# A hybrid decoder layer on one Trainium2 core: the weights of the overflow branch are loaded through the GpSimd queue instead of the SP queue

## The chip, the cores and the metric

The kernel runs on one core of one Trainium2 chip. The metric is the device time of one execution in microseconds (us). Three runs of the kernel before took 947.99, 948.39 and 949.15 us, so its median is 948.39 us. The execution that was profiled took 947.23 us, of which 945.5 us lie between its first and last instruction.

## What is computed

One decoder layer for 256 tokens of width 2048 in float32: an input projection, attention beside a convolution, an output projection, a normalisation, a mixture of experts, a second normalisation and a gated embedding. The change lies in the mixture of experts. The reference, cut to it:

```python
g_logits = t @ wg + bg                              # top-1 of 4 groups
g_top = jnp.argmax(g_logits, axis=-1)
e_in = (t @ we + be).reshape(T, 4, 8)[..., g_top]   # the 8 experts of that group
top_p, top_i = lax.top_k(softmax(e_in), 2)          # 2 experts a token
combine = ...                                       # (256 tokens, 32 experts), 2 nonzeros a row
h = jnp.einsum('td,edf->tef', t, w_gu)              # w_gu: 32 experts x 2048 x 512
act = silu(h[..., :256]) * h[..., 256:] * combine[..., None]
out = jnp.einsum('tef,efd->td', act, w_down)        # w_down: 32 experts x 256 x 2048
```

## The kernel before

**Stages.** Input projection with the convolution beside it, attention, output projection, routing, experts, second normalisation with the gate. The expert stage begins at about 400 us and ends at about 840 us.

**Experts and their places.** The 32 experts are ranked by how many tokens chose them (four of them, whose weights are fetched early, are put last). Each rank has a fixed number of places for tokens: 64 for the first four, 32 for the others. `BLOCKS` (line 44) groups ranks into nine blocks of two or four experts, so that a block fills 128 rows. For each block `gather_steps` (line 752) picks its tokens: a 0/1 table `Sb` is made on DVE, then matmuls `xpb` (line 776) multiply it into the normalised tokens, and ACT and DVE copy the result to `XTb`. `block` (line 815) then multiplies with the up weights (tile `gub`, matmul `pgb`, line 837), folds and activates (`natb`, `atb`), multiplies with the down weights (tile `dnb`, matmul `dpb`, line 898) and adds the result back to the tokens (`sob`, lines 910 to 913).

**Weights.** Every expert's weights are four `gub` and two `dnb` loads of 1 MB. `load` (line 170) issues them on the SP queue into a ring of places: 7 in one pool, 6 in a second and 2 in a third; the third is given up for block 7 (lines 1112 and 1113), which leaves 13. A load into a place waits until PE has finished with what lay there before. SP's loads also take turns on eight completion counters (named DMAHW0 to DMAHW7 in the program): a load waits until the load eight issues earlier has landed, so at most eight are under way.

**The branch for the overflow.** An expert can be chosen by more tokens than it has places. `spilled` (line 1056) counts those tokens into `flags`. Ahead of block 7 (`SPILL_BEFORE`) `spill` (line 1074) asks whether there are any; only inside that branch do 25 further branches, one for each possible overflow of a rank, gather up to 128 tokens above the places and run a `block` with one expert:

```python
with tc.If(any_ > 0):
    for i, (r, n) in enumerate(SPILL):
        with tc.If(counted(flags, 1 + i) > 0):
            for _ in gather_steps((r, P), f"o{i}", above=n): pass
            for _ in block((r, P), f"o{i}", fetch=pieces): pass
```

`fetch=pieces` (line 808) loads that expert's weights in quarters of 128 x 512. All five engines take the outer branch, each in its own instruction stream, after reading `flags` into a register (line 1071). With this input the branch's body is not run: every engine jumps to the other side of the branch, where it sets each of its counters to the value that the body would have left; ahead of that it waits for what it has issued so far on that counter. Both the jump and these waits carry line 1076 in the trace. The gather of block 7 stands behind the branch (lines 1109 and 1110), while the gathers of the other blocks are woven into the block ahead of them.

**Order of work.** The order within each engine is made by a scheduler from the program's data dependences. An engine runs its own stream strictly in order, so an instruction that waits holds all those behind it.

Of the kernel before, what the change touches and what calls it, by code (L numbers as in the profile page):

```python
# [15 lines left out]
ALU = mybir.AluOpType  # L16
AX = mybir.AxisListType
SP = mybir.EngineType.SP

P = 128  # L20
T = 256
# [6 lines left out]
NE = 32  # L28
EPG = 8
NG = 4  # L30
CH = 512
# [94 lines left out]
def tile_trunk(ctx, tc, xT, x, smalls, consts, win_m, win_v, wout, lnrows,  # L126
               gu, dn, plew, wgate, out):
    nc = tc.nc
    PE, ACT, DVE, POOL = nc.tensor, nc.scalar, nc.vector, nc.gpsimd
# [494 lines left out]
    order = rp.tile([1, NE], I32, name="order")  # L624
    comb = rp.tile([P, NT, NE], F32, name="comb")


    def sources(src):
        kind, i = src
        if kind == "static":  # L630
            return [gu[i, g] for g in range(4)], [dn[i, k] for k in range(2)]
        e = nc.values_load(order[0:1, i:i + 1], engines=[SP], min_val=0, max_val=NE - 1,
                           skip_runtime_bounds_check_because="an expert's index from a permutation")
        gs = [gu[bass.ds(e, 1), g].rearrange("o p f -> (o p) f") for g in range(4)]
        return gs, [dn[bass.ds(e, 1), k].rearrange("o p f -> (o p) f") for k in range(2)]
# [172 lines left out]
    def pieces(src, name):  # L808

        ws = [cp.tile([P, CH], F32, tag="pgs", bufs=4, name=f"{name}{k}") for k in range(4)]  # L810
        for k in range(4):
            nc.sync.dma_start(ws[k], src[:, k * CH:(k + 1) * CH])
        return ws

    def block(shape, name, done=None, fetch=whole, static=False):
        r0, M = shape
        G = P // M
        st = {128: None, 64: "st64", 32: "st32"}[M]
        srcs = [sources(("rank", r0 + e)) if not static else None for e in range(G)]

        def weights_of(kind, e, i):
            if static:
# [164 lines left out]
    with in_order():  # L987
        mvr = norm_stats(st1, bp, "n1")
        warm(W1, "r1")
        sel = selection()  # L990
        gs0 = gather_steps(BLOCKS[0], name(0), by=(pm, comb))
        b0 = block(BLOCKS[0], name(0), static=True)
        aff = first_affine()

# [52 lines left out]
        for _ in range(3):  # L1047
            next(gs1)
        next(b0)
        b1 = block(BLOCKS[1], name(1))  # L1050
        for _ in range(4):
            next(b1)
# [21 lines left out]
    def spill(flags, any_):  # L1074
# [4 lines that stand above are left out]
                    for _ in gather_steps((r, P), f"o{i}", above=n):  # L1079
                        pass  # L1080
                    for _ in block((r, P), f"o{i}", fetch=pieces):
                        pass
# [172 lines left out]
    for c in range(1, NCH):  # L1255
# [3 lines left out]
        for kt in range(KT):  # L1259
            if kt % 4 == 0:  # L1260
                w = load(wgate[c, kt // 4], f"wg{c}{kt // 4}")
            k = kt % 4
# [68 lines left out]
```

## Time and profile before

| | |
|---|---|
| three runs, us | 947.99, 948.39, 949.15 (median 948.39) |
| the profiled execution, us | 947.23 |
| its span, first to last instruction, us | 945.5 |
| mean granted clock of TensorE | 0.977 of full speed |
| PE busy | 862.3 us, 91% of the span |
| DVE busy, ACT busy, POOL busy | 509.1 us, 349.5 us, 3.0 us |
| moved by DMA | 294.44 MB, mean 311 GB/s |
| loads of `gub` in the expert stage | 112 of 1 MB, median 19.7 us from issue to landing |
| loads of `dnb` of 1 MB | 54, median 19.2 us |

PE is the engine that multiplies, PEld its weight loads, DVE, ACT and POOL (GpSimd) are the other compute engines, and SP is an engine that here issues transfers. A "q" behind a name (SPq) is that engine's stream of register, branch, wait and DMA-issuing instructions, which are not counted as busy. Times in the views count from the first instruction. "Idle before" names what ended the idle time ahead of a group of instructions. A busy PE isn't PE at its peak, and an average over the whole span mixes stages with different limits.

### The profile page before, as it was taken

The numbers are of one execution on the slowest core, as the hardware profiler recorded it, in microseconds if no ns is written. First come the engines' busy times: TensorE is split into PE (matmuls) and PEld (weight loads), VectorE is DVE, ScalarE is ACT, GpSimd is POOL, SyncE is SP. The second block draws the span as 40 slices with busy tenths as digits, with TensorE's granted clock in tenths as the row PEclk, the third lists the DMA queues.
The fourth block names the chain that finished last, engine by engine and source line by source line (L and its number), as shares of the span: only waits on it lengthen the run. The fifth ranks groups of instructions, "written<-read, shape, count | busy, mean of one in ns | idle before, by whom it ended". The sixth has DMA issues, their size and how long they took to land. (4 is left out here: it accounts for less than half of the span.)

```text
span 945.5 us, 13989 instructions
## 1 busy us (share of the span) xinstructions
PE 862.3 (91%) x5263; PEld 575.2 (61%) x5263; DVE 509.1 (54%) x1090; ACT 349.5 (37%) x684; POOL 3.0 (0%) x14
## 2 busy tenths in 40 slices
PE   7999999999999999996899989998677987989997
PEld 7999879999987877441343434432125431257886
DVE  6989998988888556540414141413032130078775
ACT  6454455566676435321111211121011211237543
POOL 0000000000000000000000000000000000000000
PEclk9999999999999999998999999999897998999999
DMA  9978855454458656899999999999979999995620
GB/s 334 368 179 242 325 203 188 140 174 152 160 179 329 264 184 271 332 420 423 424 420 423 422 421 422 421 421 424 421 316 418 420 420 422 417 418 209 217 78 33
DMA packets 44619, 294.44 MB, mean 311 GB/s; under 512 B 5160, under 2 KB 5800, under 8 KB 10240
## 3 DMA queue, kind: packets, MB, share of 16 engines
q1 hardware_dynamic: 43568, 290.85, 77.5%
q0 software_dynamic: 976, 2.63, 1.7%
q8 instruction: 43, 0.70, 0.3%
q14 instruction: 32, 0.26, 0.1%
HBM read 289.78 MB, written 3.67 MB: 310 GB/s over the span
## 5 line engine op out<-in xcount | busy, mean ns | idle before, releaser
L837 PE MATMUL pgb<-gub,XTb 128*32 128x512 f32 (+1 forms) x896 | 135.6, 621 | 22.2 <-DMA gub<-in_gu_dram 22.1
L357 DVE SCALAR_TENSOR_TENSOR yall<-u,sml,yall 128x256 f32<-128x256 f32 x240 | 108.6, 478 | 0.3
L776 PEld LDWEIGHTS xpb<-Sb,zn 128*128 128x128 f32 x576 | 71.7, 199 | 45.7 <-issue 28.7
L776 PE MATMUL xpb<-Sb,zn 128*128 128x128 f32 x576 | 81.7, 292 | 8.4 <-DVE Sb L766 7.6
L837 PEld LDWEIGHTS pgb<-gub,XTb 128*32 128x32 f32 (+1 forms) x896 | 31.6, 115 | 93.2 <-issue 50.6
L898 PE MATMUL dpb<-dnb,aTb 128*32 128x512 f32 (+1 forms) x448 | 82.6, 603 | 3.3 <-DMA dnb<-in_dn_dram 2.6
L646 DVE SCALAR_TENSOR_TENSOR atb<-atb,wb,natb 128x256 f32<-128x256 f32 x9 | 4.3, 480 | 142.2 <-ACT atb L645 142.1
L783 DVE TENSOR_SCALAR XTb<-xpb,gbc 128x128 f32<-128x128 f32 x72 | 29.5, 409 | 94.9 <-ACT XTb L781 88.7
L781 ACT ACTIVATE XTb<-xpb,gbc 128x128 f32<-128x128 f32 x72 | 33.0, 458 | 115.0 <-PE xpb L776 114.9
L177 DVE TENSOR_TENSOR Ylb<-dpb,Yhb 128x512 fp32r<-128x512 f32 x36 | 23.5, 687 | 70.8 <-ACT Yhb L176 70.8
L845 ACT COPY pgsb<-pgb 128x512 f32<-128x512 f32 x32 | 18.8, 586 | 110.4 <-PE pgb L837 108.6
L176 ACT CAST Yhb<-dpb 128x512 fp32r<-128x512 f32 x36 | 19.8, 589 | 101.7 <-PE dpb L898 98.0
L913 DVE TENSOR_TENSOR z<-z,sob 128x512 f32<-128x512 f32 x68 | 44.5, 684 | 19.3 <-PE sob L911 19.2
L898 PEld LDWEIGHTS dpb<-dnb,aTb 128*32 128x32 f32 (+1 forms) x448 | 19.5, 113 | 44.4 <-issue 35.2
L910 PE MATMUL sob<-Yhb,sctb 128*128 128x512 f32 x68 | 29.6, 467 | 17.3 <-DVE z L913 9.3
L910 PEld LDWEIGHTS sob<-Yhb,sctb 128*128 128x128 f32 x68 | 11.8, 188 | 48.2 <-ACT Yhb L176 19.1
L911 PE MATMUL sob<-Ylb,sctb 128*128 128x512 f32 x68 | 26.6, 423 | 0.0
L866 PE MATMUL natb<-pgsb,cst 128*32 128x512 f32 (+1 forms) x64 | 19.6, 659 | 4.9 <-ACT pgsb L845 4.9
L1098 PE MATMUL pl<-pw,pT 128*128 128x512 f32 x32 | 16.8, 649 | 0.0
L837 PE MATMUL pgb<-earlygu,XTb 128*32 128x512 f32 x128 | 16.5, 651 | 0.0
L911 PEld LDWEIGHTS sob<-Ylb,sctb 128*128 128x128 f32 x68 | 11.9, 191 | 5.5 <-DVE Ylb L177 5.3
L1099 ACT COPY ple<-pl 128x512 f32<-128x512 f32 x8 | 4.7, 586 | 28.5 <-PE pl L1098 28.5
(2528 smaller groups left out, 1933.8 us busy)
## 6 DMA issues: line engine op xcount, KB each, us to landing
gub<-in_gu_dram SPq DMA_DIRECT2D x112, 1024.0 KB, 19.7
dnb<-in_dn_dram SPq DMA_DIRECT2D x54, 1024.0 KB, 19.2
wo<-in_wout_dram SPq DMA_DIRECT2D x16, 1024.0 KB, 4.8
earlygu<-in_gu_dram SPq DMA_DIRECT2D x16, 1024.0 KB, 5.9
wg<-in_wgate_dram SPq DMA_DIRECT2D x16, 1024.0 KB, 6.1
wv<-in_win_v_dram SPq DMA_DIRECT2D x8, 1024.0 KB, 23.5
wk<-in_win_m_dram SPq DMA_DIRECT2D x8, 1024.0 KB, 4.8
wq<-in_win_m_dram SPq DMA_DIRECT2D x8, 1024.0 KB, 4.8
```

The source lines that it names most:

```text
L176: ACT.copy(h, src)
L177: return DVE.tensor_tensor(l, src, h.bitcast(F32), op=ALU.subtract)
L357: yield DVE.scalar_tensor_tensor(y, u[:, k:k + T], cw[:, c, k:k + 1], y, op0=ALU.mult, op1=ALU.add)
L776: PE.matmul(xp[:, k], zn[t][:, kt * P:(kt + 1) * P], S[:, t, :P], start=t == 0, stop=t == 1)
L781: ACT.activation(xs[:, 0], xp[:, 0], AF.Identity, bias=gbc[:, 1, kt:kt + 1], scale=gbc[:, 0, kt:kt + 1])
L783: DVE.tensor_scalar(xs[:, 1], xp[:, 1], gbc[:, 0, kt:kt + 1], gbc[:, 1, kt:kt + 1], op0=ALU.mult, op1=ALU.add)
L837: PE.matmul(pgs_[e][j * M:(j + 1) * M], XT[:, k, e * M:(e + 1) * M], gp[k], start=kt < G, stop=kt >= KT - G, tile_position=(0, j * M) if G ...
L866: PE.matmul(nat[e * M:(e + 1) * M], C(st), folds[e], start=True, stop=True, tile_position=(0, e * M))
L898: last = PE.matmul(dps[n][j * M:(j + 1) * M], aT[:, k, e * M:(e + 1) * M], dp[e][2 * k + n % 2], start=k == 0, stop=k == 1, tile_position= ...
L910: PE.matmul(o, table(n)[:, ts_], Yh[n], start=True, stop=False)
L911: PE.matmul(o, table(n)[:, ts_], Yl[n], start=False, stop=True)
L913: DVE.tensor_tensor(zs, zs, o, op=ALU.add)
```

## The change

The quarter loads of the overflow branch's body are issued by POOL instead of SP, and the register that holds the expert's index is loaded on POOL for that body alone. The other loads stay on SP. All 25 bodies are built with it. One import of a name apart, this is the whole diff:

```diff
+GP = mybir.EngineType.Pool
...
-    def sources(src):
+    def sources(src, by=SP):
...
-        e = nc.values_load(order[0:1, i:i + 1], engines=[SP], min_val=0, max_val=NE - 1,
+        e = nc.values_load(order[0:1, i:i + 1], engines=[by], min_val=0, max_val=NE - 1,
...
-            nc.sync.dma_start(ws[k], src[:, k * CH:(k + 1) * CH])
+            POOL.dma_start(ws[k], src[:, k * CH:(k + 1) * CH])
...
-        srcs = [sources(("rank", r0 + e)) if not static else None for e in range(G)]
+        srcs = [sources(("rank", r0 + e), GP if fetch is pieces else SP) if not static else None for e in range(G)]
```

Lines behind the new one count one more in the changed kernel (L172 becomes L173).

SP's stream between block 6 and block 7, before: the two last loads of block 6, then the branch, then (behind a body of some 1,320 rows) the far side of the branch and the first loads of block 7. `gub700` is block 7's load for expert 0, quarter 0; in brackets stand the counters that an instruction waits for.

```order
L172 DMA dnb621_6290<-in_dn_dram 128x2048 [waits DMAHW0_49,PE_49]
L172 ISA
L172 DMA dnb631_6292<-in_dn_dram 128x2048 [waits DMAHW1_49,PE_49]
L1071 TENSOR_LOAD flags_4717 [waits DVE_49]
L1076 COMPARE_AND_BRANCH
```

```order
L1076 UNCONDITIONAL_BRANCH [waits SP_sequencer_49,DMAHW0_49,DMAHW1_49,DMAHW2_49,DMAHW3_49,DMAHW4_49,DMAHW5_49,DMAHW6_49,DMAHW7_49]
L632 TENSOR_LOAD order_4142
L172 ISA
L172 DMA gub700_11963<-in_gu_dram 128x2048 [waits DMAHW2_49,PE_49]
L172 ISA
L172 DMA gub701_11972<-in_gu_dram 128x2048 [waits DMAHW3_49,PE_49]
```

The same two places of SP's stream now:

```order
L173 DMA dnb631_6292<-in_dn_dram 128x2048 [waits DMAHW1_49,PE_49]
L633 TENSOR_LOAD order_4142
L173 ISA
L173 DMA gub700_11963<-in_gu_dram 128x2048 [waits DMAHW2_49,PE_49]
L173 ISA
L173 DMA gub701_11972<-in_gu_dram 128x2048 [waits DMAHW3_49,PE_49]
L1072 TENSOR_LOAD flags_4717 [waits DVE_49]
L1077 COMPARE_AND_BRANCH
```

```order
L1079 COMPARE_AND_BRANCH
L1079 UNCONDITIONAL_BRANCH x2
L1077 UNCONDITIONAL_BRANCH [waits SP_sequencer_49]
L173 ISA
L173 DMA gub702_11978<-in_gu_dram 128x2048 [waits DMAHW4_49,PE_49]
```

On the far side SP no longer names the eight counters; two loads of block 7 stand ahead of the branch; and the body between has 75 rows instead of some 1,320. POOL's stream grew from 96 rows to 1,372, and on its far side of the branch POOL now waits for and raises the eight counters of its own queue (DMASW0 to DMASW7). ACT's copies that fold block 7 (`pgsb`, line 846 now) name those of POOL instead of SP's. A copy of ACT further on (`ple`, line 1100 now) newly names SP's eight counters, at values that they reach before block 7.

On PE the order behind the branch moved too. Before, the four products with the first weights `gub700` were finished behind 28 products of the gather (`xpb70` to `xpb76`); its last rows there:

```order
L837 MATMUL pgb70_11962<-gub700_11963,XTb70_11885 32x512 [waits DMAHW2_49]
L776 MATMUL xpb75_11918<-Sb7_11877,zn0_4128 128x128 [waits DVE_49]
L776 MATMUL xpb75_11918<-Sb7_11877,zn1_4129 128x128
...
L776 MATMUL xpb76_11925<-Sb7_11877,zn0_4128 128x128 [waits DVE_49]
L776 MATMUL xpb76_11925<-Sb7_11877,zn1_4129 128x128
...
L837 MATMUL pgb70_11962<-gub700_11963,XTb70_11885 32x512 x3
```

Now they are finished behind 16 (`xpb70` to `xpb73`), and the first product with each quarter's weights also names ACT, which copies the gathered tokens:

```order
L838 MATMUL pgb70_11962<-gub700_11963,XTb70_11885 32x512 [waits DMAHW2_49,Activation_49]
L777 MATMUL xpb72_11895<-Sb7_11877,zn0_4128 128x128 [waits DVE_49]
L777 MATMUL xpb72_11895<-Sb7_11877,zn1_4129 128x128
...
L777 MATMUL xpb73_11903<-Sb7_11877,zn0_4128 128x128 [waits DVE_49]
L777 MATMUL xpb73_11903<-Sb7_11877,zn1_4129 128x128
...
L838 MATMUL pgb70_11962<-gub700_11963,XTb70_11885 32x512 x3
L838 MATMUL pgb70_11962<-gub701_11972,XTb72_11900 32x512 [waits DMAHW3_49,Activation_49]
```

## Rows read from the trace of the kernel before

**Rows 1.** The page: busy time by engine; GB/s in 40 equal slices.

```profile
PE 862.3 (91%) x5263; PEld 575.2 (61%) x5263; DVE 509.1 (54%) x1090; ACT 349.5 (37%) x684; POOL 3.0 (0%) x14
GB/s 334 368 179 242 325 203 188 140 174 152 160 179 329 264 184 271 332 420 423 424 420 423 422 421 422 421 421 424 421 316 418 420 420 422 417 418 209 217 78 33
```

**Rows 2.** Stretches: us, PE, PEld, DVE, ACT, POOL busy (instructions), PEclk, DMA share, GB/s.

```profile
681.40:698.00 16.60, 10.72 (x55) 3.04 (x56) 3.48 (x7) 2.79 (x6) 0.00 (x0) 1.00 1.00 419
696.00:706.00 10.00, 8.55 (x41) 2.51 (x42) 4.08 (x7) 1.07 (x2) 0.00 (x0) 1.00 0.48 170
706.00:748.00 42.00, 33.56 (x230) 21.11 (x233) 11.22 (x32) 8.20 (x18) 0.00 (x0) 0.88 1.01 420
748.00:838.00 90.00, 74.91 (x397) 22.89 (x386) 16.53 (x28) 16.48 (x32) 0.00 (x0) 0.96 1.02 419
```

**Rows 3.** Line 1076, the outer branch: stream, instruction, count: ns, first and last start.

```profile
L1076 SPq EVENT_SEMAPHORE  x9: 17/17/17, 687.4 to 702.8; - x9
...
L1076 POOLq COMPARE_BRANCH  x1: 53/53/53, 420.2 to 420.2; - x1
L1076 POOLq EVENT_SEMAPHORE  x1: 17/17/17, 420.7 to 420.7; - x1
L1076 SPq COMPARE_BRANCH  x1: 50/50/50, 682.1 to 682.1; - x1
...
L1076 PEldq COMPARE_BRANCH  x1: 6265/6265/6265, 708.2 to 708.2; - x1
```

**Rows 4.** SP's own waits, 681 to 704 us: us in total, times, longest.

```profile
SPq L1076 <- SPq L1076: 20.2, 3, 12.6
```

**Rows 5.** Timeline of SP: start us, us, one issue of a load each.

```profile
641.75 0.33 SPq L172 DMA_DIRECT2D gub<-in_gu_dram  x1
...
681.40 0.33 SPq L172 DMA_DIRECT2D dnb<-in_dn_dram  x1
703.43 0.33 SPq L172 DMA_DIRECT2D gub<-in_gu_dram  x1
...
727.61 0.33 SPq L172 DMA_DIRECT2D gub<-in_gu_dram  x1
...
737.53 0.33 SPq L172 DMA_DIRECT2D dnb<-in_dn_dram  x1
741.32 0.33 SPq L172 DMA_DIRECT2D dnb<-in_dn_dram  x1
...
750.90 0.33 SPq L172 DMA_DIRECT2D gub<-in_gu_dram  x1
```

**Rows 6.** Line 172 on SP, 640 to 760 us: issue to landing.

```profile
DMA to landing us min/median/max: 4.7/19.7/22.2
```

**Rows 7.** Timeline of PE: start us, us, form and count, idle before and its releaser.

```profile
715.94 0.55 PE L776 MATMUL xpb<-Sb,zn 128*128 128x128 f32 x1 [7.60 <-DVE Sb L766]
...
776.23 3.63 PE L837 MATMUL pgb<-gub,XTb 128*32 128x512 f32 x30
786.22 1.94 PE L837 MATMUL pgb<-gub,XTb 128*32 128x512 f32 x8 [6.36 <-DMA gub<-in_gu_dram]
788.09 2.08 PE L1098 MATMUL pl<-pw,pT 128*128 128x512 f32 x2
...
802.07 1.07 PE L837 MATMUL pgb<-gub,XTb 128*32 128x512 f32 x8
803.62 1.06 PE L837 MATMUL pgb<-gub,XTb 128*32 128x512 f32 x8 [0.48 <-DMA gub<-in_gu_dram]
806.19 1.07 PE L837 MATMUL pgb<-gub,XTb 128*32 128x512 f32 x8 [1.51 <-DMA gub<-in_gu_dram]
```

**Rows 8.** PE's waits for DMA, 806 to 945 us: us in total, times, longest.

```profile
PE pgb L837 <- DMA gub<-in_gu_dram: 1.5, 1, 1.5
```

**Rows 9.** Two stretches of 2 us, columns as in Rows 2.

```profile
442.00:444.00 2.00, 1.80 (x8) 0.07 (x6) 0.00 (x0) 0.14 (x1) 0.00 (x0) 0.50 1.01 422
450.00:452.00 2.00, 2.00 (x8) 0.92 (x5) 0.06 (x1) 0.00 (x0) 0.00 (x0) 0.50 0.99 414
```

## The prediction

> **What bounds the kernel now.** I read the 40 slices of the page first. From slice 18 to slice 36 the DMA rate stands at 417 to 424 GB/s, with one dip to 316 in slice 30, from 685 to 709 us [rows 1]. So the expert stage streams weights at one steady rate, and something broke the stream once. The rate by stretches sizes the dip: 419 GB/s from 681.4 to 698 us, 170 over the ten us from 696 to 706, 420 and 419 after it [rows 2]. At 420 GB/s those ten us would have moved what took 10 x 170 / 420 = 4.05 us, so **the hole is worth 5.95 us of transfer**.
>
> SP's timeline says who made it. SP issues a 1 MB load at 641.75 us and 16 loads later at 681.40, so one every 2.48 us; then nothing until 703.43 [rows 5]. Line 1076 names the reason: SP branches at 682.1 us, and its nine steps on the far side run from 687.4 to 702.8 [rows 3], with 20.2 us of waiting, 12.6 of it in one wait [rows 4]. A load takes a median of 19.7 us to land [rows 6], which is eight loads of 2.48: SP waits there until all eight counters have landed, although the branch's body isn't run. The stream runs empty and has to fill again.
>
> Whether a hole costs time is read from PE behind it. PE starts block 7's gather at 715.94 us, held by its own jump (6.27 us) and the table from DVE [rows 3, 7]. It then works through a backlog without waiting for a weight until 779.86 (776.23 + 3.63), waits 6.36 us for the next weights, and then 0.48 and 1.51 us, the last one ending at 806.19 [rows 7]. From there to the end PE waits for no other transfer [rows 8]. So **three waits of 8.35 us in all are what later weights cost**, and everything behind 806.19 hangs on that landing.
>
> **The change, part by part.**
>
> *SP's far side.* The eight counters go to POOL. SP keeps one count of its own, and two loads of block 7 now stand ahead of the branch; they go out at the steady pace, about 683.9 and 686.4 us. SP then jumps. Its price lies between 0.5 us (POOL jumped over a body of some 75 rows, 420.2 to 420.7) and 5.3 us (SP's old body of 1,325 rows, 682.1 to 687.4) [rows 3]; SP's body now has 75 rows, so I take 0.5. Either is covered: with eight loads under way the stream lasts 19.7 us. I cost it at nothing; without that cover it would be 0.5 to 5.3 us.
>
> *The stream.* Without the hole every later load lands earlier. The lower bound is 5.95 us, from bytes. The upper one is from issues: block 8's first load goes out at 750.90 us [rows 5]; 25 issues of 2.48 us behind 681.40 would be 743.4, which is 7.5 us earlier. At 750.90 the loads under way were further along than the pace suggests, because SP had just caught up behind a full ring; bytes don't depend on that. **I take 6.0 us** and keep 7.5 for the range.
>
> *The ring.* A stream that runs ahead may find no place. Thirteen places are left in block 7, so its 14th load needs the place of its first. Before, the 14th went out at 727.61 us, the 17th at 737.53 and the 18th at 741.32 [rows 5], each when PE let a place go. In an unbroken stream block 7's k-th load lands at 681.40 + 19.7 + 2.48k: the 14th at 735.8, the 17th at 743.3, the 18th at 745.7. The fastest landing took 4.7 us [rows 6]; from the old issue times these loads can land by 732.3, 742.2 and 746.0. So even if PE let places go no earlier than before, only 0.3 us would be lost. PE's new order helps: the first weights are done behind 16 products of the gather instead of 28, and products of the gather went at 0.55 us each or faster [rows 7]. I cost the ring at nothing; for each us that PE were later here, up to one us of the gain goes.
>
> *PE.* Its start at 715.94 stays, since its jump, DVE's and the end of block 6 stay. It reaches 779.86 as before. The next weights land at 786.22 - 6.0 = 780.2, a wait of 0.4 instead of 6.36. The work from there to 803.14 (802.07 + 1.07) took 16.9 us, at the low clock in its first 4 us: eight products took 1.94 us at 786.22, 1.07 at 802.07 [rows 7]. It ends at 795.3 to 797.1, with that clock back or not, and the next weights land at 803.62 - 6.0 = 797.6, the last at 800.2. PE waits for both, so the end moves by the stream's 6.0, and neither the clock nor PE's waits for ACT (which the new order names) move it while they stay under 3 us.
>
> *POOL and ACT.* POOL's jump gets long, 5 to 6 us by those of SP and PE [rows 3]. It stands at 420.2, 320 us ahead of block 7's folds, which now wait for POOL's counters; POOL has 14 instructions of 3.0 us in the whole span [rows 1]. ACT's copy that newly names SP's counters asks for values reached by 702.8: a few steps of 17 ns [rows 3]. The bodies' loads cost nothing, since they aren't run.
>
> **Sum:** -6.0 us. Against the profiled execution's own 947.23 us that is 941.2. The median of the runs shown, 948.39, is 1.16 above that execution; what will be measured should be near **942.4 us**.
>
> **The rivals.**
>
> *The queue doesn't matter* (948.4). The Trainium skill, "DMA: Bandwidth & Descriptors", section "Issuing engines are not separate DMA queues", says that transfers started by SP, ACT or GpSimd run on the same 16 engines, so another issuing engine saves only the time of issuing. As a mechanism here: an issue takes 0.33 us [rows 5], and of the moved ones none is issued, so 0 us come back. Against it speaks that SP's 20.2 us aren't issuing but waiting for landings [rows 4], and that the wait is gone from SP's stream. It could still hold if the wait came back at SP's next loads: they name the counters one by one. But each of those had landed eight issues earlier, as everywhere in the steady stream.
>
> *The hole moves* (943.4 to 945.4). PE could let places go 1 to 3 us later than I reckon, since its products with weights now stand between the gather's and wait for ACT. Then the stream stalls around 740 us, and the gain is 3 to 5 us. For it speaks the thin margin of the 17th and 18th load, against it the new order.
>
> *The clock takes half* (944 to 946.5). Before, the 6.36 us wait brought PE to the low clock. The new waits near 796 to 800 us are shorter (0.5 to 2.3 and 1.5 us), but if the clock fell there, PE sets the pace behind them. The longest low stretch among the experts (granted 0.50, 1.2 of 2.4 GHz) lasted 10 us (442 to 452) [rows 9]; products then take 1.94 instead of 1.07, so 45% of it is lost, 4.5 us at most.
>
> *Slower* (above 950.3). The same mechanism, further on: if the low clock held from 800 us for longer than 7.9 / 0.45 = 17.5 us, the loss would pass the 6.0 gained and 1.9 more. No stretch of the expert stage lasted that long, which speaks against it; that PE alone sets the pace from 806 to the end speaks for it.
>
> **How the numbers follow.** About 0.2%, 1.9 us, can be told from no change, so "faster" begins below 946.5 and "slower" above 950.3. Chances: the forecast 0.74 (its own range 940.9, with 7.5 us gained, to 943.2); the hole moves 0.08; the clock takes half 0.08, nearly all of it still faster; no change 0.07; slower 0.03. That makes 0.89 faster, 0.08 same, 0.03 slower. The range runs from 940.6, the upper bound of the gain and a little of the runs' spread, to 945.8, which takes in the moved hole and most of the clock's case.
>
> **What would show it.** Right: no gap in SP's issues near 682 to 703 us beyond a few us, no dip in slice 30, line 1077 on SP with one step instead of nine, PE's wait near 780 us under 1 us, the weights that landed at 806.19 landing near 800, and PE's start of block 7 still near 716. Wrong: DMA below 400 GB/s between 715 and 760 us (the ring), a low clock behind 800 us, or a new wait of SP behind the branch. The whole falls if PE reaches the products of 806.19 late for a reason other than weights.

## The result and the profile after

The changed kernel takes **943.55 us** (median of five runs, 942.33 to 944.71) against 949.15 us (947.99 to 950.65) for the kernel before, run on the same chip. The ratio is **0.9946 [0.9935, 0.9958]**, a gain of 5.6 us. The forecast was 942.4 us with a range of 940.6 to 945.8 and 0.89 on faster. The profiled execution took 943.01 us, of which 941.3 us are its span, at a mean granted clock of 0.979.

The page of the changed kernel: busy time by engine and GB/s in 40 equal slices (they answer to [rows 1]):

```profile
PE 861.2 (91%) x5263; PEld 573.2 (61%) x5263; DVE 508.5 (54%) x1090; ACT 349.5 (37%) x684; POOL 3.0 (0%) x14
...
GB/s 331 374 175 246 322 199 194 142 180 139 175 176 309 290 140 256 332 423 422 422 421 423 421 421 423 421 423 423 421 422 416 420 423 420 417 416 204 219 79 33
```

The engines do the same work: PE's busy time differs by 1.1 us in 862. What changed stands in slice 30, which moved 316 GB/s before and moves 422 now. The stretch that held the hole [rows 2] now runs at the steady rate; its columns are as there:

```profile
696.00:706.00 10.00, 8.11 (x41) 2.17 (x39) 3.65 (x7) 0.78 (x3) 0.00 (x0) 1.00 1.02 422
```

The outer branch is line 1077 now. Its rows (stream, instruction, count: ns, first and last start) answer to [rows 3]:

```profile
L1077 POOLq EVENT_SEMAPHORE  x5: 17/43/43, 427.3 to 427.7; - x5
L1077 POOLq COMPARE_BRANCH  x1: 53/53/53, 421.9 to 421.9; - x1
L1077 POOLq INC_SWDGE_SEM  x1: 220/220/220, 427.8 to 427.8; - x1
L1077 SPq COMPARE_BRANCH  x1: 50/50/50, 688.8 to 688.8; - x1
L1077 SPq EVENT_SEMAPHORE  x1: 17/17/17, 689.3 to 689.3; - x1
...
L1077 PEldq COMPARE_BRANCH  x1: 6096/6096/6096, 709.1 to 709.1; - x1
```

SP has one step on the far side instead of nine, 0.5 us behind its branch. The long jump is POOL's now: 421.9 to 427.3 us. SP's waits from 681 to 712 us (us in total, times, longest) answer to [rows 4]:

```profile
SPq L173 <- DMA dnb<-in_dn_dram: 14.3, 8, 2.0
SPq L173 <- DMA gub<-in_gu_dram: 7.5, 4, 1.9
SPq L1077 <- SPq L1077: 0.5, 1, 0.5
```

SP still waits for landings, 21.8 us in twelve waits, but never over 2.0 us and for one counter at a time: that is the steady pace, in which each landing lets one load go. The 20.2 us in three waits, 12.6 the longest, are gone. The issues of a load each, from SP's timeline, answer to [rows 5]: the last load of block 6, the first three of block 7, its 14th, its 17th and block 8's first.

```profile
683.13 0.33 SPq L173 DMA_DIRECT2D dnb<-in_dn_dram  x1
685.62 0.33 SPq L173 DMA_DIRECT2D gub<-in_gu_dram  x1
688.09 0.33 SPq L173 DMA_DIRECT2D gub<-in_gu_dram  x1
690.58 0.33 SPq L173 DMA_DIRECT2D gub<-in_gu_dram  x1
...
724.66 0.33 SPq L173 DMA_DIRECT2D gub<-in_gu_dram  x1
...
734.19 0.33 SPq L173 DMA_DIRECT2D dnb<-in_dn_dram  x1
...
748.58 0.33 SPq L173 DMA_DIRECT2D gub<-in_gu_dram  x1
```

The pace of 2.48 us goes through the branch without a break. PE's timeline around the weights that set the end answers to [rows 7]:

```profile
716.42 3.75 PE L777 MATMUL xpb<-Sb,zn 128*128 128x128 f32 x16 [7.18 <-DVE Sb L767]
...
775.54 3.64 PE L838 MATMUL pgb<-gub,XTb 128*32 128x512 f32 x32
782.33 1.74 PE L838 MATMUL pgb<-gub,XTb 128*32 128x512 f32 x8 [3.15 <-DMA gub<-in_gu_dram]
784.00 2.08 PE L1099 MATMUL pl<-pw,pT 128*128 128x512 f32 x2
...
799.73 1.07 PE L838 MATMUL pgb<-gub,XTb 128*32 128x512 f32 x8 [0.48 <-DMA gub<-in_gu_dram]
802.30 1.07 PE L838 MATMUL pgb<-gub,XTb 128*32 128x512 f32 x8 [1.51 <-DMA gub<-in_gu_dram]
```

The wait that ended at 806.19 ends at 802.30, 3.89 us earlier. PE's start of block 7 hardly moved: 716.42 against 715.94.

Why 3.9 and not 6? In this execution the stream was late before it reached the branch: block 6's last load went out at 683.13 us, before at 681.40. **Measured from that load, the weights of 802.30 come 3.89 + 1.73 = 5.62 us earlier.** A part of the lateness can be seen at 322 to 340 us, long before the experts. The same stretch, first of the kernel before, then of the changed one (columns as in [rows 2]):

```profile
322.00:340.00 18.00, 18.00 (x109) 15.65 (x108) 8.46 (x13) 6.20 (x11) 0.00 (x0) 1.00 0.38 124
```

```profile
322.00:340.00 18.00, 18.00 (x102) 15.50 (x101) 7.50 (x12) 5.61 (x10) 0.00 (x0) 0.91 0.34 117
```

A mean granted clock of 0.91 over 18 us gives away 0.09 x 18 = 1.6 us, an estimate that fits what follows: the cast of `order` on DVE (line 719 before, 720 now), which stands behind that stretch, starts at 363.9 us before and at 365.5 in the changed kernel. The change touches nothing there, and among the experiments below the same stretch shows 1.00, 0.91 or 0.81 in kernels of either kind. So it belongs to the execution, not to the change.

### The profile page after: what moved, and what is told of

The parts are those of the page before. It is cut to its first block, busy times and chain, and to the rows that moved or that the text cites. A ratio compares the mean times of both kernels' runs of the same rounds, so it can differ in the third digit from the quotient of the medians.

```text
span 941.3 us, 13999 instructions
## 1 busy us (share of the span) xinstructions
PE 861.2 (91%) x5263; PEld 573.2 (61%) x5263; DVE 508.5 (54%) x1090; ACT 349.5 (37%) x684; POOL 3.0 (0%) x14
## 5 line engine op out<-in xcount | busy, mean ns | idle before, releaser
L838 PE MATMUL pgb<-gub,XTb 128*32 128x512 f32 (+1 forms) x896 | 138.3, 632 | 19.5 <-DMA gub<-in_gu_dram 19.5
```

The lines of the kernel that those rows point to most:

```text
L838: PE.matmul(pgs_[e][j * M:(j + 1) * M], XT[:, k, e * M:(e + 1) * M], gp[k], start=kt < G, stop=kt >= KT - G, tile_position=(0, j * M) if G ...
```

## The experiments

**Theory.** What came back is the hole in the weight stream, and the hole came from SP's wait for all eight landings on the far side of the branch. **Rivals:** the long jump over SP's old body (5.3 us), the two loads that now stand ahead of the branch together with PE's new order, another queue as such, or PE's and DVE's own jumps.

**1. One of the 25 bodies on SP again.** The other 24 stay on POOL.

```diff
-                    for _ in block((r, P), f"o{i}", fetch=pieces):
+                    for _ in block((r, P), f"o{i}", fetch=pieces_sp if i == 0 else pieces):
```

> Theory A (the waits): the time came from the eight landings that SP waited for on the far side of the branch; here one of the 25 bodies loads through SP again, so the eight waits are back while SP's body stays short (192 instructions in the branch against 2,219 before and 102 in the changed kernel). A expects the time of before, 948 to 950 us, a gap of about 22 us in SP's issues and about 6 us of DMA transfer lost near 700 us. Theory B (the jump): the time came from SP's long body, whose jump took 5.3 us; B expects the time of the changed kernel, 942.5 to 945 us, and no gap. Theory C (the order: two loads of block 7 ahead of the branch, and PE's new order behind it) expects the time of before too, since in this kernel both orders are the old ones.

Measured: 949.25 us (12 runs) against 948.11 for the kernel before, ratio 1.0004 [0.9995, 1.0014]. Its branch rows, its wait and its stretch:

```profile
L1083 SPq EVENT_SEMAPHORE  x9: 17/17/17, 688.1 to 703.6; - x9
...
L1083 SPq COMPARE_BRANCH  x1: 50/50/50, 682.9 to 682.9; - x1
```

```profile
SPq L1083 <- SPq L1083: 20.3, 3, 12.5
```

```profile
696.00:706.00 10.00, 8.53 (x41) 2.50 (x42) 4.07 (x7) 1.20 (x3) 0.00 (x0) 1.00 0.48 175
```

The last weights, on PE:

```profile
806.92 1.06 PE L844 MATMUL pgb<-gub,XTb 128*32 128x512 f32 x8 [1.52 <-DMA gub<-in_gu_dram]
```

One body that isn't run brings back all of it: nine steps, 20.3 us of waiting, 175 GB/s. Block 6's last load went out at 682.15 us, so the last weights come 124.77 us behind it, against 806.19 - 681.40 = 124.79 us in the kernel before and 802.30 - 683.13 = 119.17 us in the changed one. One body on SP with the eight counters in it is enough. But the two hoisted loads fall back behind the branch too, and SP's jump is again 5.2 us, so this run alone doesn't separate the theory from the first two rivals.

**2. A long body on SP without loads.** All loads stay on POOL; SP gets four register reads a quarter load, which name no counter.

```diff
+PAD = 4
...
+            for _ in range(PAD):
+                nc.values_load(order[0:1, 0:1], engines=[SP], min_val=0, max_val=NE - 1,
...
```

> All bodies load through POOL as in the changed kernel, but every quarter load is followed by four loads of a register on SP, so that SP's body in the branch is longer than before (2,527 instructions against 2,219). A: no change from the changed kernel, 942.5 to 945 us; SP's jump takes 5 to 6 us again, but eight loads under way cover it, no dip of the DMA rate. B: the time of before, 948 to 950 us. C: 942.5 to 945 us, since the orders are the new ones.

Measured: 941.95 us, ratio 0.9929 [0.9917, 0.9941]. The jump is long, the stream whole:

```profile
L1081 SPq COMPARE_BRANCH  x1: 50/50/50, 688.5 to 688.5; - x1
L1081 SPq EVENT_SEMAPHORE  x1: 17/17/17, 693.7 to 693.7; - x1
```

```profile
696.00:706.00 10.00, 7.65 (x38) 2.06 (x38) 3.17 (x5) 0.56 (x2) 0.00 (x0) 1.00 1.01 418
```

SP stands still for 5.2 us and issues nothing from 687.74 to 693.96 us, and it costs nothing: eight loads were under way, and the gain (6.2 us by the medians) is at least the changed kernel's. The long jump is refuted as the cause.

**3. The loads on ACT's queue instead of POOL's.**

```diff
-GP = mybir.EngineType.Pool
+GP = mybir.EngineType.Activation
...
-            POOL.dma_start(ws[k], src[:, k * CH:(k + 1) * CH])
+            ACT.dma_start(ws[k], src[:, k * CH:(k + 1) * CH])
```

> The bodies load through ACT's queue instead of POOL's. Their loads then use the same eight counters as SP's, and SP still waits for all eight on the far side, though its body is short (310 instructions) and two loads of block 7 stand ahead of the branch. A: the time of before, 947.5 to 950 us, with a hole of about 6 us that begins some 5 us later than before, since SP also waits for the two loads ahead. B and C: the time of the changed kernel, 942.5 to 945 us.

Measured: 947.76 us (12 runs), ratio 0.9995 [0.9985, 1.0005]: nothing gained. SP doesn't issue one load in the branch, two of block 7's loads stand ahead of it and PE has the new order, yet

```profile
L1077 SPq EVENT_SEMAPHORE  x9: 17/17/17, 694.3 to 709.3; - x9
...
L1077 SPq COMPARE_BRANCH  x1: 50/50/50, 689.1 to 689.1; - x1
```

```profile
701.00:711.00 10.00, 8.68 (x42) 2.86 (x40) 3.80 (x7) 1.07 (x2) 0.00 (x0) 0.84 0.57 219
```

SP waits for the eight counters all the same, because the loads on ACT's queue use the eight that SP's loads use; its steps there are only some 6.5 us later (the last at 709.3 instead of 702.8), and the hole with them. So neither the hoisted loads nor PE's order gives the gain, and neither does taking the loads off SP. What gives it is that POOL's loads count on **other counters**. The Trainium skill, "DMA: Bandwidth & Descriptors", section "Issuing engines are not separate DMA queues", says that another issuing engine saves only the time of issuing; this run agrees (0.9995). The 5.6 us that POOL's queue brings aren't a saving of that kind: they are time of waiting.

**4. No branch at all.** The call of the branch is taken out, and with it the work on tokens above their places.

```diff
-            spill(flags, any_)
```

> The changed kernel without the branch (tokens above the places are not computed; with this input there are none to compute, the flags are still counted). Block 7's gather stays where it was, behind block 6. If the end is set by the stream of weights, as in theory A, the jumps of PE, DVE and ACT (PE idle from 709 to 716 us) are not on the path: 941.5 to 944.5 us, and PE waits some 7 us more for weights in block 8. Rival D: the jumps are on the path, and their 7 us come off: 935 to 938 us.

Measured: 943.42 us, ratio 0.9944 [0.9931, 0.9956], the same as the changed kernel. PE starts block 7 at 709.22 us, 7 us earlier, and spends them waiting:

```profile
709.22 2.05 PE L777 MATMUL xpb<-Sb,zn 128*128 128x128 f32 x16 [0.24 <-DVE z L914]
...
780.96 1.93 PE L838 MATMUL pgb<-gub,XTb 128*32 128x512 f32 x8 [6.97 <-DMA gub<-in_gu_dram]
...
800.97 1.06 PE L838 MATMUL pgb<-gub,XTb 128*32 128x512 f32 x8 [1.50 <-DMA gub<-in_gu_dram]
```

Block 6's last load went out at 683.32 us, so the last weights come 117.65 us behind it, 1.5 us sooner than in the changed kernel; the time doesn't show that difference. The jumps of PE (6.1 us) and DVE that remain cost nothing that can be seen in the time; the stream sets the end. So in this order the branch has next to nothing left to give.

**5. How many landings may SP wait for?** A dose. The first 4, 6 or 7 quarter loads of one body go to SP. They take their turn on the counters from the oldest load under way on, so SP waits on the far side for the 4, 6 or 7 oldest of its eight landings. `ON_SP` is 4, 6 or 7, and `n` is what is left of it for this load.

```diff
+ON_SP = 4
...
-            POOL.dma_start(ws[k], src[:, k * CH:(k + 1) * CH])
+            by, s = (nc.sync, sp) if k < n else (POOL, src)
+            by.dma_start(ws[k], s[:, k * CH:(k + 1) * CH])
```

> Four quarter loads of the first body are on SP, so on the branch's far side SP waits for the four oldest of its eight landings and no more. Landings come every 2.48 us, so SP is held about 4 x 2.48 = 10 us and then has four loads still under way. Theory (what costs is only the time in which nothing is under way: the end of SP's wait plus the 4.7 us of the fastest landing, against 19.8 us from the last issue to the last landing): 9.9 + 4.7 = 14.6 is under 19.8, no dip of the rate, and the time of the changed kernel, 943 to 943.7. Rival (each us that SP is held costs its share of the 5.6 us that 22 us of holding cost before): 10 / 22 x 5.6 = 2.5 us, 945.7.

> As before with six landings: SP held about 15 us, two loads still under way. Theory: 14.9 + 4.7 = 19.6 against 19.8, just covered: 943.2 to 944.3, at most a dip of 1 us of transfer. Rival: 15 / 22 x 5.6 = 3.8 us, 947.

> Seven landings, the newest not among them: SP held about 17.5 us, one load still under way. Theory: 17.4 + 4.7 = 22.1 against 19.8, a hole of 2.3 us (up to 3.5, as the hole of 5.95 us for eight is larger than the same sum gives): 945.4 to 946.7. Rival: 17.5 / 22 x 5.6 = 4.5 us, 947.7.

SP's steps on the far side number 5, 7 and 8 in the three kernels, one more than the landings waited for; with seven, its branch stands at 684.1 us:

```profile
L1083 SPq EVENT_SEMAPHORE  x5: 17/17/17, 684.0 to 693.0; - x5
```

```profile
L1083 SPq EVENT_SEMAPHORE  x7: 17/17/17, 683.1 to 696.6; - x7
```

```profile
L1083 SPq EVENT_SEMAPHORE  x8: 17/17/17, 684.6 to 701.1; - x8
...
L1083 SPq COMPARE_BRANCH  x1: 50/50/50, 684.1 to 684.1; - x1
```

Against 949.02 us for the kernel before on that chip:

| landings waited for | us | ratio | SP's last issue ahead of the branch to its first behind | from that last issue to the last weights, us |
|---|---|---|---|---|
| 4 | 943.03 | 0.9939 [0.9920, 0.9957] | 682.75 to 693.64 | 119.19 |
| 6 | 942.55 | 0.9934 [0.9920, 0.9947] | 681.91 to 697.22 | 118.80 |
| 7 | 946.01 | 0.9962 [0.9949, 0.9974] | 683.40 to 701.76 | 121.23 |
| 8 (experiment 1, another chip) | 949.25 | 1.0004 [0.9995, 1.0014] | 682.15 to 704.19 | 124.77 |

The last column ends where PE starts on the last weights, in the kernels with 4, 6 and 7:

```profile
801.94 1.07 PE L844 MATMUL pgb<-gub,XTb 128*32 128x512 f32 x8 [1.45 <-DMA gub<-in_gu_dram]
```

```profile
800.71 1.07 PE L844 MATMUL pgb<-gub,XTb 128*32 128x512 f32 x8 [1.50 <-DMA gub<-in_gu_dram]
```

```profile
804.63 1.06 PE L844 MATMUL pgb<-gub,XTb 128*32 128x512 f32 x8 [1.51 <-DMA gub<-in_gu_dram]
```

The stretches of 5 us from 696 to 706 us, of the runs with 4, 6 and 7:

```profile
696.00:701.00 5.00, 4.35 (x22) 1.42 (x24) 3.57 (x6) 0.07 (x1) 0.00 (x0) 1.00 1.01 423
701.00:706.00 5.00, 4.15 (x28) 0.95 (x20) 0.49 (x1) 1.08 (x2) 0.00 (x0) 1.00 1.02 419
```

```profile
696.00:701.00 5.00, 4.60 (x24) 1.38 (x24) 2.23 (x4) 0.00 (x0) 0.00 (x0) 1.00 0.96 385
701.00:706.00 5.00, 3.80 (x18) 1.00 (x16) 1.83 (x3) 1.07 (x2) 0.00 (x0) 1.00 1.01 421
```

```profile
696.00:701.00 5.00, 3.70 (x11) 1.07 (x8) 3.06 (x5) 1.07 (x2) 0.00 (x0) 0.84 0.89 370
701.00:706.00 5.00, 5.00 (x28) 1.34 (x29) 0.88 (x2) 0.00 (x0) 0.00 (x0) 0.74 0.78 257
```

SP may be held for 15.3 us (six landings) at no cost that can be seen; the rate only dips to 385. At seven the holes add up to 5 x (1 - 370/421) + 5 x (1 - 257/421) = 2.6 us, and the time rises by 3.0 to 3.5 us over the other two. The intervals of the times with four and seven overlap; the last column, which leaves out how late an execution reached the branch, separates them: 2.0 and 2.4 us more with seven than with four and six, and 5.6 to 6.0 more with eight. At eight the whole gain is gone. The rival by which each held microsecond costs its share asked for 945.7 and 947 us with four and six; both are refuted. In all three of these kernels block 7's first loads stand behind the branch again, and PE has the old order (it starts with 40 products of the gather, as before); with four and six the gain is there all the same, so neither is needed for it. **The cost is the time in which too little is under way, and it sits in the last two landings of eight.**

**6. Is anything left?** In the changed kernel PE still waits 5.5 us for weights between 780 and 803 us, and the embedding's products (`pl`, line 1099), which need no weights of the experts, stand partly behind those waits. `share, total` says how they are woven into block 8's steps: its parts are spread over 16 of them, and in the experiments over 12, 8 and 6.

```diff
-            side, share, total = embedding(gp_), 5, 16
+            side, share, total = embedding(gp_), 5, 12
```

> The changed kernel once more, as the base for the two orders of the embedding sent with it. Both theories: 943.5 us median, 0.994 to 0.996 of the kernel before; no dip of the DMA rate near 700 us; PE's waits for weights near 780 to 802 us add up to 2 to 6 us, by how late that execution's stream stands.

> If the stream's last weights set the end of the experts behind the change (PE still waits 5.5 us for weights near 780 to 802 us), PE work that is done in these waits instead of behind them comes for nothing: some 4 of the 16 pl groups move ahead of the last weights, and the time falls by 1 to 3 us against the changed kernel, to 940.5 to 942.5. Rival 1 (PE's own work behind 802 us does not set the end, e.g. the chain through DVE and the second normalisation does): no change, 943 to 944. Rival 2 (pw or pT land too late for the earlier place, or the places of the ring come free later): PE waits longer near 790 us and it is slower by 0.5 to 2 us.

> The embedding spread over half of block 8's steps instead of all of them. By the first theory as much as the 12-step order or a little more, 940 to 942.5, since PE has only about 5 us of waits to fill: what is moved beyond that delays block 8's products and frees places later. Rival 1: no change, 943 to 944. Rival 2: slower than the 12-step order, the weights then land later or PE sets the pace.

> The embedding's products still earlier (over 6 of the steps instead of 8). If PE's waits for weights were all that there was to fill, nothing is left to gain: within 0.7 us of the 8-step order, 940.5 to 941.6. Rival (moved work now delays the products that free places, so the stream itself falls back): PE waits longer for weights behind 800 us and it is 1 us or more slower than the 8-step order, 942 or above.

> The 8-step order once more, to have the kernel that is ahead of the changed one on more executions: 940.9 median, 0.991 to 0.993 of the kernel before. If its first result was chance, it falls back to the changed kernel's 943.2 to 943.6, 0.9945 or above.

| | us | ratio to the kernel before | PE's waits for weights, 770 to 842 us |
|---|---|---|---|
| the changed kernel again | 943.15 | 0.9946 [0.9928, 0.9964] | 6.1 |
| 12 | 941.86 | 0.9932 [0.9914, 0.9949] | 3.0 |
| 8 | 940.92 | 0.9919 [0.9903, 0.9936] | 3.3 |
| 8, more runs | 941.28 | 0.9921 [0.9906, 0.9936] | 3.8 |
| 6 | 940.74 | 0.9916 [0.9901, 0.9931] | 4.2 |

The last `pl` ends near 814 us in the changed kernel and near 800 with 8 steps. Line 1099 by form (count: min/median/max ns, first and last start), of the changed kernel again and of the 8-step order:

```profile
L1099 PE MATMUL pl<-pw,pT x32: 592/592/1222, 783.7 to 813.4; 128*128 128x512 f32 x32
```

```profile
L1099 PE MATMUL pl<-pw,pT x32: 592/592/697, 779.7 to 799.6; 128*128 128x512 f32 x32
```

With 8 steps the first of them starts where PE had waited, and none runs at 1222 ns, the price at the low clock: the long wait after which the clock had fallen is filled. How much of the gain is the filled wait and how much the clock isn't separated here. By the medians the 8-step order is about 2 us ahead of the changed kernel, and the 6-step order adds nothing that can be told from it. The intervals of the changed kernel and of the reordered ones overlap, so this second gain is less sure than the first. Against the kernel before, the orders with 8 and 6 steps are 7.1 to 7.7 us faster.

## Why the prediction was right, point by point

*The hole, 6.0 us.* Right in mechanism and in size. By the medians the gain is 5.6 us, and 5.0 us where the changed kernel was run again (experiment 6). From block 6's last load to the last weights it is 5.62 us in the profiled execution (124.79 - 119.17) and 5.99 us with six landings (124.79 - 118.80). The count by bytes (5.95) was the right one for a kernel that keeps the branch. The 7.5 us by issues were not reached there; without the branch, where the loads of block 7 stay on the pace for longer, the stream comes 124.79 - 117.65 = 7.14 us earlier, though the time doesn't follow. The dose bears the mechanism out: with seven landings a hole of 2.6 us cost 3.0 to 3.5 us.

*SP's far side at nothing.* Right. The jump took 0.5 us, and experiment 2 shows that 5.2 us would have cost nothing either.

*The ring at nothing.* Right. The 13 places ran out where the prediction said: the 14th load went out at 724.66 us instead of on the 2.48 us pace, and the 17th at 734.19, but slices 31 to 36 stayed at 416 to 423 GB/s, so the rival in which the hole moves didn't occur. Without the branch, where PE starts block 7 some 7 us earlier, the 14th load went out at 718.19 us, on the pace, and the last weights came 1.5 us sooner in the stream. So a full ring may have cost a little there; no run separates it, and no time shows it.

*PE.* The landings were foreseen at 780.2, 797.6 and 800.2 us; they came at 782.33, 799.73 and 802.30, each 2.1 us later, as much as the stream's lateness of 1.73 us explains and 0.4 more. With six landings, where block 6's last load went out only 0.51 us later than before, the first and the last came at 780.74 and 800.71. The sign that the prediction named, a wait under 1 us near 780, didn't show. One size was off: the wait at 780 was to be 0.4 us and was 3.15. The step that failed is that PE "reaches 779.86 as before", with weights landing at 780.2: PE was through at 779.18 (775.54 + 3.64), 0.7 us sooner although it had started 0.5 us later, and the weights came 2.1 us after the forecast. It cost nothing, since PE waits for the next weights anyway; but it brought the low clock back, which the prediction had counted as a possibility at that place. Two `pl` products took 2.08 us at 784.00, the same as at 788.09 before. The granted clock was 0.50 (1.2 GHz) from 784 to 786 us and 1.00 again from there on, so the rival in which the clock takes half didn't occur.

*POOL and ACT at nothing.* Right. POOL's jump took 5.4 us where 5 to 6 were foreseen, 290 us ahead of block 7.

*The queue doesn't matter.* In experiment 3 this rival is exactly what happens: on ACT's queue it gives 0.9995. It failed here for the reason that the prediction gave against it, that SP was not issuing but waiting; what the prediction did not say is that another queue alone would not do, since ACT's loads share the counters of SP's.

*Time.* The median of 943.55 us lies 1.15 us above the 942.4 forecast. The kernel before had a median of 949.15 beside this result and 948.39 in the runs that the forecast started from, which is 0.8 us of it.

## What to carry to other kernels

A branch that isn't run can still cost: in this kernel its far side waits until every counter that the body uses has come to rest (nine steps with eight counters, five with four), and on the queue that feeds the kernel this empties the pipeline. Look for it as a dip in one slice of the DMA rate with a branch line on SP beside it, size it in bytes, and move the body's loads to counters that nobody else is using at that point; another engine alone isn't enough. A held queue is harmless while enough is under way, so ask which landing the wait is for, not how long it lasts. What the body's loads cost on POOL's queue when the branch is taken is not shown: with this input no run takes it.

## What had not been expected

**SP's jump had two prices.** Its branch to the far side took 0.5 us over a body of 139 instructions as built (seven landings: 684.1 to 684.6 us) and over 102 (the changed kernel, whose 75 rows put repeated instructions together), but 5.2 us over 192 (experiment 1) and 5.2 over 310 and 2,527 (experiments 3 and 2). Above 192 it doesn't grow with the length. Where between 139 and 192 the step lies was not tried. The Trainium skill, "Runtime: NRT & Kernel Launch", section "Instruction fetch mechanics", says that a taken branch forces a fetch of the target when that lies outside the two pages that are loaded. The two prices of SP, 0.5 and 5.2 us, fit a fetch that is needed or not, but no run here shows the fetch itself. Length alone doesn't set the price on ACT: its jump took 5.3 us in the changed kernel (705.9 to 711.2) and 2.4 in experiment 3 (707.8 to 710.2), where its body is the longer one (2,399 instructions as built against 605).

**Loads of SP and ACT share counters in this kernel** (experiment 3), so a body that uses one queue holds the other.

**The stretch at 322 to 340 us ran at a mean clock of 1.00 in four of the fourteen profiled executions, 0.91 in nine and 0.81 in one**, though nothing that these kernels change lies there. At 0.91 that is 1.6 us, more than a quarter of the whole effect of the change, in a single profile. A difference between two profiled executions should be measured from an event just ahead of the change.
